# A new stream order for a hybrid decoder step, and a second copy of the last norm's scale

## The chip, the cores and the metric

The kernel runs on one core of one Trainium2 chip. The metric is the device time of one execution in microseconds (us). Three runs of the kernel before took 565.85, 564.5 and 568.01 us, median 565.85 us. All times of the trace come from one further execution, the profiled one, whose own time was 564.84 us.

## The reference

One inference step of a one-layer decoder over 256 prompt tokens and 64 sample tokens (8 sequences of 8 tokens, each with 1024 cached positions in 8 pages). Everything is float32.

```python
h = rms_norm(x, g_mix)
qa, ka, va, qs, ks, vs, ga, gs = split(h @ w_in)          # 1024 -> 5120
o_a = moba_block(rope(qa), rope(ka), va)                  # block-sparse softmax, branch 0
o_s = stick_breaking_block(qs, ks, vs)                    # branch 1
x = x + (sigmoid(ga) * (o_a @ w_branch_moba) + sigmoid(gs) * (o_s @ w_branch_sb)) @ w_out
h2 = rms_norm(x, g_ffn)
x = x + (silu(h2 @ w_ffn_gate) * (h2 @ w_ffn_up)) @ w_ffn_down
y = rms_norm(x, g_final)
```

For the sample tokens the keys and values of each branch are the cached pages (found through `page_table`) followed by the new rows. The results are `y` and the new keys and values.

## The kernel before

Activations are kept transposed, as 8 tiles of 128 features by T = 320 tokens. Every dense product is made from two roundings of each operand: a weight tile `wr` is loaded by a DMA of the SP queue (512 KB, line 157), split by ScalarE into `wh` (L152) and by VectorE into the rest `wl` (L153), and multiplied as xh·wh + xl·wh + xh·wl (L344 for the query, key and gate tiles, 24 matmul records each; L185 elsewhere). There are 3 raw buffers `wr` and 3 pairs of split ones.

The sample tokens attend to the cache in **units**: a unit is two of the eight sequences of one branch, so there are four units per branch. A unit needs four loads of cached keys (`kr`, about 1.05 MB each, four DMAs of the SP queue at L533, after a load of page numbers at L529) and four gathers of cached values (`vr`, 1.05 MB each, indirect DMAs issued by GpSimd at L541). Keys and values share one ring of 7 buffers (`RB`), so a load waits until the step that used the buffer seven loads earlier is done. Before each gather GpSimd copies one element of the key load issued last but one (`seen`, L540, `LAG` = 2); since GpSimd works in order, this holds the gather back until those keys have landed.

Up to the merge of the two branches the work is cut into steps of six **streams**, and the string `ORDER` says which stream makes its next step:

- `d`: dense work: query and key tiles, values of new tokens, first branch's output product
- `g`: gate tiles
- `s`: scores of a unit against its cached keys, in two halves (L571)
- `a`: three steps per unit: transposes of the probabilities (L659, L667; called keys step below), then the two halves of the product with the cached values (L691, 32 and 40 matmul records)
- `e`: end of a unit: its output transposed back (L704)
- `p`: attention of the prompt tokens: two score steps (L463), transposes (L504), product (L518), for two groups of heads per branch

A function is called per letter, and after each step `Loads.feed` issues what has become possible: splits of weights, one cache load at most (`PACE`), and weight loads. The list of loads follows the same string. The orders of TensorE, GpSimd and the SP queue are exactly the program's; ScalarE and VectorE are ordered by the scheduler. So a letter moved in `ORDER` moves matmuls, and with them the moments at which buffers are released and the places of DMAs in the SP queue.

After the streams come the merge, the output projection, the feed-forward part and the last norm (`last_norm`). There the scale `r` of 128 x 320 elements (the same in all partitions) is made by ScalarE and three VectorE operations, and the 8 output tiles are `xg * r`: six single tiles on VectorE, two together on GpSimd (all L854); each is then stored by a DMA of the SP or the ScalarE queue (L855).

The table of the order and the loop that reads it:

```python
for c in ORDER:
    gen, (after, mark) = self.steps.pop(c)
    ...
    step = next(gen, None)
    ...
    self.loads.feed()
```

Of the kernel before, what the change touches and what calls it, by code (L numbers as in the profile page):

```python
# [6 lines left out]
F32 = mybir.dt.float32  # L7
F32R = mybir.dt.float32r
I32 = mybir.dt.int32
AF = mybir.ActivationFunctionType  # L10
ALU = mybir.AluOpType
# [3 lines left out]
P = 128  # L15
# [4 lines left out]
T = NP_ + NS  # L20
# [13 lines left out]
SB, TB, OB, DB = 2, 3, 1, 2  # L34
# [15 lines left out]


ORDER = (
    "dddddddsddddsddsaddpsaadasegdsdaaapeddsadpsggdaappeaapdddssp"
    "gpepdgddpsagasapggegapaapgpsseggpggpdsagdasaaedgaaded"
)


# [82 lines left out]
class Net:  # L140
# [697 lines left out]
    def last_norm(self, acc, xg):  # L838

        nc, y, x1 = self.nc, self.stg, self.x1  # L840
        ps = self.pp.tile([P, T], F32, name="rb", tag="o", bufs=OB)
        nc.tensor.matmul(ps, self.ones, acc[:, 0], start=True, stop=False)
        for c in (slice(0, T // 2), slice(T // 2, T)):
            nc.tensor.matmul(ps[:, c], self.ones, acc[:, 1, c], start=False, stop=c.stop == T)
        r, w = [y.tile([P, T], F32, name=n, tag="y", bufs=3) for n in ("r", "w")]
        nc.scalar.activation(r, ps, AF.Abs_reciprocal_sqrt, scale=1.0 / D)
        nc.vector.tensor_mul(w, r, r)
        nc.vector.scalar_tensor_tensor(w, w, -0.5 / D, ps, op0=ALU.mult, op1=ALU.mult)
        nc.vector.scalar_tensor_tensor(r, w, 1.5, r, op0=ALU.add, op1=ALU.mult)
        e = 0  # L850
        for i, n in enumerate((1, 1, 1, 1, 1, 1, 2)):
            s = slice(e, e + n)
            engine = nc.gpsimd if i == 6 else nc.vector
            engine.tensor_tensor(x1[:, s], xg[:, s], r[:, None, :].to_broadcast([P, n, T]), ALU.mult)  # L854
            (nc.scalar if i % 2 else nc.sync).dma_start(self.O["y"][:, s], x1[:, s])  # L855
            e += n

# [185 lines left out]
```

## Time and profile before

| what | value |
|---|---|
| median of three runs | 565.85 us |
| profiled execution, own time | 564.84 us |
| its span | 563.0 us |
| TensorE busy | 543.2 us (96%) |
| VectorE, ScalarE, GpSimd busy | 332.7, 268.7, 48.8 us |
| HBM read | 134.22 MB |
| mean granted TensorE clock | 0.986 of full speed |

The span is what lies between the first and the last event of the core; the execution's own time is 1.8 us longer. The streams take the first 275 us of the span; in the rest TensorE is busy almost without a gap. In the profile, PE is TensorE, DVE is VectorE, ACT is ScalarE, POOL is GpSimd and SP the engine that issues most DMAs; PEclk is the share of the full clock that was granted to TensorE. A row of waits reads: total us, number of times, longest.

### The profile page before, as it was taken

Reading aid. Unit: us, or ns where it says so; the run is one execution under the profiler, and the core shown is the slowest. Engines: PE = TensorE matmul, PEld = TensorE weight load, DVE = VectorE, ACT = ScalarE, POOL = GpSimd, SP = SyncE. Lnnn points to the kernel's source line nnn. Section 1 sums busy time; section 2 is a strip of 40 time slices with the busy share of each in tenths; the row PEclk is TensorE's granted clock in tenths of the full one; section 3 lists DMA queues with packets and bytes.
Section 4 is the critical chain, followed back from the end, with each engine's and each line's share of the span. In section 5 each row is a group of like instructions: output and inputs, shape, how many; then the busy total and the mean of one; then the engine's idle time right before and its main releaser. Section 6 shows DMA issues by size and latency. Waiting matters only on the chain.

```text
span 563.0 us, 10934 instructions
## 1 busy us (share of the span) xinstructions
PE 543.2 (96%) x4252; PEld 494.0 (88%) x4252; DVE 332.7 (59%) x600; ACT 268.7 (48%) x483; POOL 48.8 (9%) x73
## 2 busy tenths in 40 slices
PE   8899999799999999999999999999999999999992
PEld 6888867578778787977999999999999999999992
DVE  6777675255575746764688656666666665444434
ACT  7775555325675444643446454444444443354321
POOL 0002102140021402131000000000000000000001
PEclk9899999799999999999999999999999999999997
DMA  8899999999699999987595544444444444544512
GB/s 306 296 374 331 368 358 405 413 392 400 225 363 357 352 401 351 383 316 293 198 325 162 150 130 151 146 150 154 149 146 152 150 152 140 153 141 144 161 33 93
DMA packets 45571, 138.86 MB, mean 247 GB/s; under 512 B 5200, under 2 KB 7504, under 8 KB 41296
## 3 DMA queue, kind: packets, MB, share of 16 engines
q1 hardware_dynamic: 40336, 104.06, 54.4%
q0 software_dynamic: 4608, 33.56, 15.0%
q8 instruction: 33, 0.54, 0.4%
q10 hardware_dynamic: 576, 0.56, 0.3%
q14 instruction: 18, 0.15, 0.1%
HBM read 134.22 MB, written 3.93 MB: 245 GB/s over the span
## 4 chain that ended last, share of the span: by engine, by line
PE 81%; DMA 7%; ACT 5%; DVE 3%; SPq 2%; issue 1%; DVEq 0%; POOL 0%; ACTq 0%
PE dps L185 55%; PE dps L344 12%; PE S L571 4%; PE po L691 4%; DMA vr<-in_cv,small 3%; DMA wr<-in_w_in 2%; ACT rot L363 2%; DMA kr<-in_ck 1%; PE dps L388 1%; PE tp L667 1%; PE dps L518 1%; PE tp L504 1%; ACT wh L152 1%; PE dps L463 1%; DVE wl L153 1%
## 5 line engine op out<-in xcount | busy, mean ns | idle before, releaser
L152 ACT ACTIVATE wh<-wr 128x1024 fp32r<-128x1024 f32 (+1 forms) x122 | 127.0, 1045 | 187.0 <-issue 110.9
L153 DVE TENSOR_TENSOR wl<-wr,wh 128x1024 fp32r<-128x1024 f32 (+1 forms) x122 | 146.8, 1205 | 76.9 <-ACT wh L152 76.7
L185 PE MATMUL dps<-x1h,wh 128*128 128x320 f32 x352 | 109.0, 310 | 0.0
L185 PE MATMUL dps<-x1l,wh 128*128 128x320 f32 x352 | 108.8, 309 | 0.0
L185 PE MATMUL dps<-x1h,wl 128*128 128x320 f32 x352 | 108.8, 309 | 0.0
L344 PE MATMUL dps<-xs,wh 128*128 128x320 f32 x256 | 78.5, 319 | 1.6 <-ACT wh L152 1.4
L344 PE MATMUL dps<-xl,wh 128*128 128x320 f32 x256 | 77.2, 314 | 0.2 <-DVE xl L307 0.2
L185 PEld LDWEIGHTS dps<-x1h,wh 128*128 128x128 f32 x352 | 66.1, 188 | 0.1
L185 PEld LDWEIGHTS dps<-x1l,wh 128*128 128x128 f32 x352 | 66.1, 188 | 0.0
L185 PEld LDWEIGHTS dps<-x1h,wl 128*128 128x128 f32 x352 | 66.1, 188 | 0.0
L185 PE MATMUL dps<-fh,wl 128*128 128x320 f32 x176 | 54.4, 309 | 0.0
L185 PE MATMUL dps<-fh,wh 128*128 128x320 f32 x176 | 54.4, 309 | 0.0
L185 PE MATMUL dps<-fl,wh 128*128 128x320 f32 x176 | 54.4, 309 | 0.0
L344 PEld LDWEIGHTS dps<-xs,wh 128*128 128x128 f32 x256 | 48.7, 190 | 4.7 <-ACT wh L152 1.5
L344 PEld LDWEIGHTS dps<-xl,wh 128*128 128x128 f32 x256 | 48.8, 191 | 0.9 <-DVE xl L307 0.9
L344 PE MATMUL dps<-xs,wl 128*128 128x320 f32 x256 | 43.6, 310 | 0.0
L344 PEld LDWEIGHTS dps<-xs,wl 128*128 128x128 f32 x256 | 39.3, 189 | 0.3 <-DVE wl L312 0.3
L541 POOL DMA_INDIRECT vr<-in_cv,small x32 | 33.3, 1040 | 43.1 <-PE po L691 11.4
L691 PE MATMUL po<-vr,pt 128*32 128x256 f32 x512 | 32.3, 394 | 4.4 <-DMA vr<-in_cv,small 4.4
L185 PEld LDWEIGHTS dps<-fh,wh 128*128 128x128 f32 x176 | 33.0, 188 | 0.0
L185 PEld LDWEIGHTS dps<-fl,wh 128*128 128x128 f32 x176 | 33.0, 188 | 0.0
L185 PEld LDWEIGHTS dps<-fh,wl 128*128 128x128 f32 x176 | 33.0, 188 | 0.0
(203 smaller groups left out, 848.9 us busy)
## 6 DMA issues: line engine op xcount, KB each, us to landing
kr<-in_ck SPq DMA_DIRECT2D x128, 256.0 KB
wr<-in_w_ff SPq DMA_DIRECT2D x44, 512.0 KB
wr<-in_w_in SPq DMA_DIRECT2D x30, 512.0 KB
wr<-in_w_down SPq DMA_DIRECT2D x16, 448.0 KB
wr<-in_w_v SPq DMA_DIRECT2D x8, 512.0 KB
wr<-in_w_b SPq DMA_DIRECT2D x8, 512.0 KB
wr<-in_w_out SPq DMA_DIRECT2D x8, 512.0 KB
wr<-in_w_down SPq DMA_DIRECT2D x8, 512.0 KB
```

The lines of the kernel that those rows point to most:

```text
L152: self.nc.scalar.activation(hi, raw, AF.Copy)
L153: self.nc.vector.tensor_tensor(lo, raw, r32(hi), ALU.subtract)
L185: nc.tensor.matmul(ps, w, x, start=first and i == 0, stop=last and i == len(todo) - 1)
L344: self.nc.tensor.matmul(ps, a, x, start=k + low + i == 0, stop=low == 1 and k + n == KD and i == n - 1)
L363: nc.scalar.activation(rot[32 * q:32 * q + 32], ps[32 * s:32 * s + 32], AF.Copy)
L388: nc.tensor.matmul(ps, self.xs[:, k], w[k][j], start=k + j == 0, stop=k + j == KD)
L463: nc.tensor.matmul(S[e][:, i], q[r, 2 * u + i, half * P:half * P + P], k[r, 2 * u + i, half * P:NP_], start=True, stop=True)
L504: nc.tensor.transpose(tp[:, i * P:(i + 1) * P], src, self.ident)
L518: nc.tensor.matmul(po[r, i, :NP_ if kt else P], t["v"][:, kt, c0:c0 + HD], mv, start=kt == 1, stop=kt == 0)
L541: self.nc.gpsimd.indirect_dma_start(out=raw.rearrange("p a b -> p (a b)"), out_offset=None, in_=self.I[f"cv{br}"], in_offset=bass.Indirect ...
L571: nc.tensor.matmul(S[r], QS[:, hp, r], raw[x][:, :, hp * P:(hp + 1) * P], start=i == 0, stop=i == 1)
L691: nc.tensor.matmul(po[r], PT[j][:, r], v[:, c:c + 256], start=j == 0, stop=j == 8)
```

## The change

Two edits. The string `ORDER` has the same letters in another order from its 19th to its 66th step. In unit 0 of the first branch, the values are multiplied directly after the scores of unit 1, ahead of a query tile of the second branch that stood there; a prompt score step moves from behind the values of unit 1 to ahead of them; the transposes of unit 2 move behind more dense work; a gate tile moves ahead of the new-value projection of the second branch. Which loads are made, and the sequence of the cache loads among themselves, stay the same; weight loads change places with them.

In `last_norm`, ScalarE copies the scale `r` into a PSUM bank (`rb`, tag `s`, which the attention scores used before). The first VectorE product still reads `r` in SBUF, the five others read the copy in the bank, GpSimd's product reads `r` in SBUF.

```diff
 ORDER = (
-    "dddddddsddddsddsaddpsaadasegdsdaaapeddsadpsggdaappeaapdddssp"
-    "gpepdgddpsagasapggegapaapgpsseggpggpdsagdasaaedgaaded"
+    "dddddddsddddsddsadpsaadasegpddsdaapdedspadasggdaappeaagdddss"
+    "pgpepdddpsagasapggegapaapgpsseggpggpdsagdasaaedgaaded"
 )
...
         nc.vector.scalar_tensor_tensor(r, w, 1.5, r, op0=ALU.add, op1=ALU.mult)
+
+        rb = self.pp.tile([P, T], F32, name="rstd3", tag="s", bufs=SB)
+        nc.scalar.activation(rb, r, AF.Copy)
         e = 0
         for i, n in enumerate((1, 1, 1, 1, 1, 1, 2)):
             s = slice(e, e + n)
-            engine = nc.gpsimd if i == 6 else nc.vector
-            engine.tensor_tensor(x1[:, s], xg[:, s], r[:, None, :].to_broadcast([P, n, T]), ALU.mult)
+            engine, v = (nc.gpsimd, r) if i == 6 else (nc.vector, rb if i else r)
+            engine.tensor_tensor(x1[:, s], xg[:, s], v[:, None, :].to_broadcast([P, n, T]), ALU.mult)
             (nc.scalar if i % 2 else nc.sync).dma_start(self.O["y"][:, s], x1[:, s])
```

On TensorE, behind the new-value projection of the first branch (`dps_903`), there stood before the query tile `dps_929` of the second branch, the prompt scores (L463), the scores `S` of unit 1 (L571, with its own keys at L615), the values `po` of unit 0 (L691) and the next query tile `dps_1108`:

```order
L344 MATMUL dps_929<-xs,wh_688 128x320
...
L344 MATMUL dps_929<-xs,wl_689 128x320 x8
L463 MATMUL dps_961<-kT_233,qT_232 128x256
...
L571 MATMUL S_984<-kr_458,QS_226 32x512 x2
...
L615 MATMUL own_995<-kT_233,QS_226 32x8 x8
L691 MATMUL po_1041<-vr_653,pt_880 32x256 x2
...
L691 MATMUL po_1041<-vs_235,pto_873 32x256 x4
L344 MATMUL dps_1108<-xs,wh_814 128x320
```

Now the same place reads, up to the first scores of unit 2 (`S_1134`):

```order
L463 MATMUL dps_923<-kT_233,qT_232 128x256
...
L571 MATMUL S_946<-kr_458,QS_226 32x512 x2
...
L615 MATMUL own_957<-kT_233,QS_226 32x8 x8
L691 MATMUL po_1003<-vr_653,pt_880 32x256 x2
...
L691 MATMUL po_1003<-vs_235,pto_873 32x256 x4
L344 MATMUL dps_1076<-xs,wh_688 128x320
...
L344 MATMUL dps_1076<-xs,wl_689 128x320 x8
L659 MATMUL tp_1111<-ident,pown_970 128x128
...
L571 MATMUL S_1134<-kr_889,QS_225 32x512 x2
```

The query tile has moved from ahead of the prompt scores to behind the values of unit 0, and one query tile fewer stands ahead of the scores of unit 2.

In the SP queue, behind the first of the four key loads of unit 2 (`kr_889`), stood a weight load `wr_959`, then the second and third key load (`kr_1027`, `kr_1058`):

```order
L157 DMA wr_827<-in_w_in 128x1024
L529 TENSOR_LOAD small
...
L533 DMA kr_889<-in_ck 128x512
...
L157 DMA wr_959<-in_w_in 128x1024
...
L533 DMA kr_1027<-in_ck 128x512
...
L533 DMA kr_1058<-in_ck 128x512
```

Now the key loads follow each other, and the weight load (`wr_1109`) comes behind the fourth:

```order
L157 DMA wr_827<-in_w_in 128x1024
L529 TENSOR_LOAD small
...
L533 DMA kr_889<-in_ck 128x512
...
L533 DMA kr_989<-in_ck 128x512
...
L533 DMA kr_1020<-in_ck 128x512
...
L533 DMA kr_1056<-in_ck 128x512
L157 DMA wr_1109<-in_w_in 128x1024
```

One weight load has moved behind three key loads; the third of them (`kr_1058` before, `kr_1020` now) is the one that GpSimd's `seen` copies read ahead of the four gathers of unit 1.

At the end of the program, ScalarE now has these rows; before, the third was not there:

```order
L246 ACTIVATE acc_5639<-x_3741 128x160 x2
L831 ACTIVATE xg<-x_3741,small 128x320
L846 ACTIVATE r<-rb 128x320
L852 ACTIVATE rstd_6371<-r 128x320
L858 DMA out_y<-x_3741 128x320 x3
```

The copy stands ahead of the three stores in ScalarE's queue.

## Prediction

> **What bounds the kernel now.** I read the page first, then TensorE's waits, then the timeline around the longest of them.
>
> ```profile
> span 563.0 us, 10934 instructions
> ...
> PE 543.2 (96%) x4252; PEld 494.0 (88%) x4252; DVE 332.7 (59%) x600; ACT 268.7 (48%) x483; POOL 48.8 (9%) x73
> ```
>
> TensorE sets the time: 19.8 us of the span are all that it is not busy. The change takes no matmul away, so it can only win what TensorE waits or runs slowly, and what lies behind its last matmul. Its waits, in total, times, longest:
>
> ```profile
> PE po L691 <- DMA vr<-in_cv,small: 4.4, 2, 3.5
> PE dps L344 <- ACT wh L152: 1.4, 1, 1.4
> ```
>
> The largest is a product with cached values that waits for its gather. TensorE's timeline shows where (start, duration):
>
> ```profile
> 95.36 1.93 PE L691 MATMUL po<-vr,pt 128*32 128x256 f32 x32
> 98.16 0.62 PE L691 MATMUL po<-vr,pt 128*32 128x256 f32 x4 [0.87 <-DMA vr<-in_cv,small]
> 102.31 1.51 PE L691 MATMUL po<-vr,pt 128*32 128x256 f32 x12 [3.53 <-DMA vr<-in_cv,small]
> ```
>
> These are the values of unit 1: the first half runs through, the second finds its third gather just late and its fourth very late. What that costs is more than the idle 4.4 us, as stretches with PE busy, granted clock and DMA show:
>
> ```profile
> 95.36:102.31 6.95, 2.56 (x37) 1.08 (x36) 2.04 (x5) 4.29 (x15) 2.29 (x4) 0.82 1.01 413
> 102.31:106.69 4.38, 4.38 (x37) 1.75 (x37) 0.00 (x0) 0.00 (x0) 0.00 (x0) 0.51 1.04 423
> 20.00:25.00 5.00, 4.52 (x20) 4.52 (x21) 4.02 (x8) 2.79 (x5) 0.00 (x0) 0.66 0.59 197
> 65.00:75.00 10.00, 10.00 (x131) 6.95 (x133) 8.34 (x18) 4.47 (x10) 0.00 (x0) 1.00 0.87 316
> 75.00:86.84 11.84, 11.84 (x97) 9.73 (x90) 6.88 (x23) 7.98 (x25) 3.25 (x6) 1.00 1.02 373
> 140.00:145.00 5.00, 5.00 (x61) 3.26 (x63) 3.61 (x8) 3.14 (x7) 0.00 (x0) 1.00 0.17 43
> ```
>
> After the wait the clock was granted by half (0.51), and the rest of the step took twice its time. The chain of waits prices the step without a wait, and shows the queues ahead of it:
>
> ```profile
> 67.83 0.33 SPq L157
> ...
> 69.33 0.34 SPq L533
> ...
> 71.37 0.37 SPq L157
> 71.78 0.88 SPq L529
> 72.93 0.33 SPq L533
> ...
> 88.11 14.16 DMA vr<-in_cv,small
> 102.31 4.44 PE po L691 x36
> ...
> 107.89 0.30 PE dps L463
> 108.53 0.37 PE tp L704 x2
> 108.90 7.04 PE dps L344 x48
> ...
> 117.80 1.73 PE po L691 x32
> ...
> 137.25 2.30 PE po L691 x40
> ```
>
> An undisturbed first half takes 1.73 us and a second half 2.30. Starting at 95.36, unit 1 would have ended at 99.39; it ended at 102.31 + 4.44 = 106.75. **The loss is 7.4 us**, and it is the most that the new order can win there.
>
> The gathers were late because they were held back. GpSimd's timeline, of the last gather of unit 0 and of the gathers of unit 1:
>
> ```profile
> 62.57 0.97 POOL L541 DMA_INDIRECT vr<-in_cv,small  x1 [5.18 <-PE tp L659]
> 82.69 0.18 POOL L540 COPY seen<-kr 1x1 f32<-1x1 f32 x1 [19.16 <-DMA kr<-in_ck]
> 83.43 0.97 POOL L541 DMA_INDIRECT vr<-in_cv,small  x1 [0.56 <-issue]
> ...
> 84.75 0.97 POOL L541 DMA_INDIRECT vr<-in_cv,small  x1 [0.16 <-issue]
> ...
> 88.11 0.97 POOL L541 DMA_INDIRECT vr<-in_cv,small  x1 [0.16 <-issue]
> ```
>
> All four wait for the third key load of unit 2 to land (82.69); the fourth is issued at 88.11 and lands 14.16 us later into DMA engines that are full (1.01 and 1.04 above).
>
> **The change: the stream order.** Three moves matter.
>
> *TensorE's arrival.* These two rows of the timeline give the old places of unit 0's values and of unit 2's first scores:
>
> ```profile
> 71.71 3.64 PE L691 MATMUL po<-vr,pt 128*32 128x256 f32 x64
> ...
> 80.41 1.92 PE L571 MATMUL S<-kr,QS 128*32 128x512 f32 x16
> ```
>
> A query tile costs 3.52 us (7.04 for 48 records). One tile fewer stands ahead of both, so TensorE gets to unit 0's values at 68.2 and to unit 2's scores at 76.9. Ahead of unit 1's values stand all the same steps and one prompt score step more (0.64, from 107.89 to 108.53): 96.0 in place of 95.36, if nothing else waits.
>
> *The keys.* SP issued the first key load of unit 2 at 69.33, the weight load at 71.37, the second key load at 72.93. Without the weight load the second follows 0.4 us sooner (0.37 and its gap). Its buffer comes from unit 1's scores, and they are done 3.5 us earlier than before, so that no wait is added on SP. In the DMA queue 0.52 MB fall away ahead of it, 1.4 us at the 373 GB/s of that stretch. So the third key load lands between 0.4 and 1.8 us sooner; I take 1.5, nearer the sum since the DMA engines are busy there: the gate opens at 81.2.
>
> *The gathers.* After the gate the first was issued 0.74 later, and the next 1.32 after it. With the same steps the fourth goes at 81.2 + 0.74 + 3 x 1.32 = 85.9, 2.2 sooner; its buffer, held by the first keys of unit 2, is released by unit 2's scores before 80.5. How fast it lands depends on who shares the engines. While the gathers ran, from 87 to 93 us, the queues of GpSimd (first row) and SP moved, in packets and MB:
>
> ```profile
> q0 software_dynamic: 247, 1.89, 74.7%
> q1 hardware_dynamic: 317, 0.58, 26.5%
> ```
>
> So a loaded SP queue leaves the gathers three quarters. The competitors are the same keys of unit 3 and weights, some a little earlier, plus the displaced weight load, which lands ahead of the gathers. I keep the 14.16 us: the fourth gather is there at 100.0, bounds 99.6 (another 0.4 from the keys that are served earlier) and 101.3 (the gate gains 0.4 and half the rest is eaten by the displaced load).
>
> *What becomes late next.* TensorE comes to unit 2's scores at 76.9 with two key loads issued only from 69.33 on. With the tail of the weight load of 67.83 they are 2.6 MB; at the 316 GB/s of this stretch that is 8.3 us, so about 77.6. Besides, the exponentials of unit 1, which the keys step needs, queue behind two weight splits of VectorE and ScalarE that used to run ahead of the scores. Neither wait is in the old trace; the one bound is zero, the other 3.5 us (the keys were there at 80.41 without a wait). I take 0.9 us for both, close to the estimate of the landing. Unit 0's fourth gather, issued at 62.57, must now be there at 68.2 + 1.73 + 0.2 = 70.1, 7.5 us after its issue; the old place shows no wait at 73.6, so the wait is between zero and 3.5; its engines had only SP's weights beside it, and I take zero.
>
> Then unit 1's values start at 96.9, the second half at 98.6, its fourth gather is wanted at 98.8 and there at 100.0: a wait of 1.2. The half ends 2.1 later, at 102.1. In the old trace this point, with the prompt step added, was 106.75 + 0.64 = 107.4. **The stream order wins 5.3 us**; the bounds are 7.4 (no wait) and 2.5 (first rival). Later steps get more lead: from 102 to 140 the old PE waited for nothing, and the DMA engines stood idle at 140 to 145 (0.17), so there is room to serve a TensorE that runs 5 us earlier. The output and feed-forward phases behind move as a block.
>
> **The change: the last norm.** Six rows carry it: ScalarE's `r`, two VectorE operations, GpSimd's product, and the chain at its end.
>
> ```profile
> 553.30 0.44 ACT L846 ACTIVATE r<-rb 128x320 f32<-128x320 f32 x1 [0.22 <-PE rb L844]
> ...
> 554.37 0.49 DVE L848 SCALAR_TENSOR_TENSOR w<-w,rb 128x320 f32<-128x320 f32 x1
> ...
> 555.70 1.60 POOL L854 TENSOR_TENSOR x<-xg,r 128x640 f32<-128x640 f32 x1 [299.98 <-DVE r L849]
> ...
> 555.83 1.82 DVE L854 TENSOR_TENSOR x<-xg,r 128x320 f32<-128x320 f32 x1
> ...
> 555.91 1.74 DVEq L1021
> 557.64 1.61 DVE x L854 x4
> ```
>
> VectorE's second product takes 1.82 us where the last four take 1.61 together: it stands while GpSimd's product runs (555.70 to 557.30). [...] An operation that reads the bank costs 0.49 (`w<-w,rb`), no more than others. ScalarE's copy costs about the 0.44 of `r`, from 555.41 to 555.87, under the first product, which keeps `r` in SBUF for that; ScalarE has nothing else, and its three stores are queued behind the copy but wait for later products anyway. Then five products run from 555.91: at 0.40 each to 557.9, at 0.49 + 0.03 to 558.5, against 559.25 (557.64 + 1.61). That is 1.3 or 0.7; I take **1.1**. GpSimd's half (557.30) is done before; its store goes behind SP's others and moves with them.
>
> **The sum.** Own time of the profiled execution 564.84 - 5.3 - 1.1 = 558.4. The median lies 1.0 above that execution; part of the spread of the three runs (3.5 us) should come from the wait that shrinks, so I add half: **558.9**.
>
> **The rivals.**
>
> *The wait stays and halves the clock again.* The gather gains only to 101.3, unit 1 waits 2.5 us, and the following 3.4 us run at half speed, which costs another 1.5: end at 101.3 + 2.1 + 1.5 = 104.9, won 2.5, with the norm 3.6. Time 561.7 (again with 0.5 for the median). For it: the engines are full, and the order cannot add bandwidth; after waits of 1.4 us and less near 20 us the clock was 0.66. [...] Chance 0.27.
>
> *The norm's copy frees nothing.* If GpSimd holds VectorE back also when one input lies in a bank, or the copy comes late, the norm wins 0: 560.0. Against it stands the duration of the bank-reading row, but GpSimd was idle then. Chance 0.09.
>
> *Slower.* TensorE now runs closer to its transfers in four places between 68 and 100 us (unit 0's values, keys step, unit 2's scores, unit 1's values). If each short wait takes the clock down, half speed could hold over most of that stretch. A halved stretch of 3.4 us loses 1.7; from the fifth on, the old loss of 7.4 and the norm's 1.1 are outweighed. With six: 10.2 and waits of 0.9, unit 1 ends at 96.0 + 11.1 + 4.0 = 111.1, 3.7 later than before; minus 1.1, time 567.9. Against it: in the trace one long wait gave one stretch of half clock, and after it 1.00. Chance 0.05.
>
> **How the numbers follow.** The forecast has 0.59; its own range is 557.0 (no wait left, median as profile) to 560.2. About 1% (5.7 us) is what a measurement of this kernel can tell from no change; faster by over 1% means below 560.2. Faster: nearly all of the forecast's cases (0.55), half of the second rival (0.04): 0.59. Slower by over 1% would be above 571.5, beyond even the price of the last rival: 0.02. Within 1%: the rest, 0.39. The range takes in the best case, 564.84 - 7.4 - 1.3 = 556.1, and the first rival with 1 us for the median: 556.2 to 562.6.
>
> **What would show it.** Right: TensorE's waits for `vr` fall from 4.4 to about 1.2; the clock of the stretch around unit 1's second half is above 0.9; GpSimd's gathers of unit 1 are issued from 82 to 86; a new wait of under 1.5 us at the scores of unit 2 or the keys step ahead of it; VectorE's second product takes about 0.5 and the last ends some 3 us after `r`. Wrong: a fourth gather still issued after 87.5, a new wait over 1.5 us at unit 0's values, a wait for `vr` or `kr` behind 107 us that gives the win back, or a second product that still takes over 1.5.

## The result, and the profile after

The changed kernel takes 559.34 us (median; 558.54 to 560.11) against 566.31 us for the kernel before, timed beside it. The ratio is 0.9877, with a 95% interval of 0.9841 to 0.9913: 1.2% faster. The prediction said 558.9 us and held the time in its range. The profiled execution took 558.79 us, 6.05 less than the one of before (564.84).

The page of the changed kernel, first its head, then TensorE's wait for the gathers of values (total us, times, longest):

```profile
span 557.0 us, 10934 instructions
...
PE 541.3 (97%) x4252; PEld 493.6 (89%) x4252; DVE 331.3 (59%) x600; ACT 269.4 (48%) x484; POOL 45.7 (8%) x73
```
```profile
PE po L691 <- DMA vr<-in_cv,small: 0.9, 1, 0.9
```

This wait has fallen from 4.4 us to 0.9. Two small waits are new, in brackets in the timeline below: for the probabilities (`p`) at the keys step of unit 1, and for the keys (`kr`) at unit 2's scores. Besides, TensorE's own busy time is 1.9 us shorter with the same 4252 matmuls: those of unit 1's second half run at the full clock where they ran at half. The stretches around these places (PE, PEld, DVE, ACT and POOL busy, granted clock, DMA share, GB/s):

```profile
75.00:80.00 5.00, 4.42 (x31) 2.09 (x29) 2.97 (x8) 2.99 (x9) 0.00 (x0) 1.00 0.93 343
...
100.00:105.00 5.00, 4.06 (x52) 2.75 (x51) 1.61 (x5) 2.28 (x6) 2.29 (x4) 1.00 1.05 413
```

The clock is 1.00 in both; before it was 0.51 from 102.31 to 106.69. From 100 to 105 us the DMA engines are as full as they were (1.05 against 1.06); from 75 to 80 us they are a little less so (0.93 against 1.02, 343 GB/s against 391). TensorE's timeline of the changed kernel, at the keys step and unit 2's scores, and at unit 1's values:

```profile
75.62 0.27 PE L659 MATMUL tp<-ident,pown 128*128 128x128 f32 x1
76.24 1.09 PE L667 MATMUL tp<-ident,p 128*128 128x128 f32 x8 [0.35 <-ACT p L642]
77.27 1.05 PE L571 MATMUL S<-kr,QS 128*32 128x512 f32 x4
78.55 1.91 PE L571 MATMUL S<-kr,QS 128*32 128x512 f32 x12 [0.23 <-DMA kr<-in_ck]
80.39 0.44 PE L704 MATMUL tp<-ident,o 128*128 128x128 f32 x2
...
97.85 2.35 PE L691 MATMUL po<-vr,pt 128*32 128x256 f32 x36
101.14 1.71 PE L691 MATMUL po<-vr,pt 128*32 128x256 f32 x26 [0.94 <-DMA vr<-in_cv,small]
...
103.42 1.53 PE L504 MATMUL tp<-ident,z 128*128 128x128 f32 x12
```

The idle times in brackets understate what such a wait costs, because the ends of matmuls are modelled and a loosely spaced group counts as busy. Counted from start to start, the keys step takes 77.27 - 75.62 = 1.65 us against 1.08 before, and the first half of unit 2's scores 80.39 - 77.27 = 3.12 against 1.86 when it waits for nothing. Unit 1's values end at 103.42, where the prediction's equivalent of the old trace stood at 107.4.

GpSimd's timeline shows when the gathers of unit 1 go, and the chain of waits how long the fourth takes:

```profile
81.32 0.18 POOL L540 COPY seen<-kr 1x1 f32<-1x1 f32 x1 [17.98 <-DMA kr<-in_ck]
82.06 0.97 POOL L541 DMA_INDIRECT vr<-in_cv,small  x1 [0.56 <-issue]
...
85.66 0.39 POOL L540 COPY seen<-kr 1x1 f32<-1x1 f32 x1
86.21 0.97 POOL L541 DMA_INDIRECT vr<-in_cv,small  x1 [0.16 <-issue]
```
```profile
86.21 14.88 DMA vr<-in_cv,small
```

The gate opens 1.37 us sooner than before (82.69), and the fourth gather goes 1.9 sooner (88.11). It takes 14.88 us to land, 0.7 longer than before.

Of the 1.9 us by which the gather goes sooner, 0.5 does not come from the gate. Before, the `seen` copy ahead of the fourth gather took 0.91 us, while VectorE split a weight tile, an operation with two SBUF inputs:

```profile
86.69 1.22 DVE L153 TENSOR_TENSOR wl<-wr,wh 128x1024 fp32r<-128x1024 f32 x1
```
```profile
87.03 0.91 POOL L540 COPY seen<-kr 1x1 f32<-1x1 f32 x1
```

The split ends at 87.91, the copy at 87.94. In the changed kernel such a split ends at 86.02 and the copy, of 0.39 us, at 86.05. Seven of the twelve traces of this case have a copy of 0.39 to 0.96 us at this place, the other five one of 0.18. Whether the split is what lengthens it was not tested.

At the end of the program, the rows of VectorE, ScalarE and GpSimd:

```profile
549.55 0.49 DVE L848 SCALAR_TENSOR_TENSOR w<-w,rb 128x320 f32<-128x320 f32 x1
550.08 0.49 DVE L849 SCALAR_TENSOR_TENSOR r<-w,r 128x320 f32<-128x320 f32 x1
...
551.08 2.08 DVE L857 TENSOR_TENSOR x<-xg,rstd 128x320 f32<-128x320 f32 x5
...
550.60 0.44 ACT L852 ACTIVATE rstd<-r 128x320 f32<-128x320 f32 x1 [1.68 <-DVE r L849]
...
550.88 1.61 POOL L857 TENSOR_TENSOR x<-xg,r 128x640 f32<-128x640 f32 x1 [300.00 <-DVE r L849]
```

Five products from the bank take 2.08 us together, and none stands still while GpSimd's product runs (550.88 to 552.49). The row `w<-w,rb` divides the whole gain in two: it starts 4.82 us earlier than before (554.37), which is what the new order won, and the span ends 7.45 after it instead of 8.63, which is what the last norm won: 1.2.

### The profile page after: what moved, and what is told of

It reads as the page before. It is cut to its first block, busy times and chain, and to the rows that moved or that the text cites. A ratio compares the mean times of both kernels' runs of the same rounds, so it can differ in the third digit from the quotient of the medians.

```text
span 557.0 us, 10934 instructions
## 1 busy us (share of the span) xinstructions
PE 541.3 (97%) x4252; PEld 493.6 (89%) x4252; DVE 331.3 (59%) x600; ACT 269.4 (48%) x484; POOL 45.7 (8%) x73
## 4 chain that ended last, share of the span: by engine, by line
PE 85%; DMA 6%; ACT 3%; DVE 2%; SPq 2%; issue 1%; POOL 1%; DVEq 0%; POOLq 0%; ACTq 0%
PE dps L185 56%; PE dps L344 12%; PE po L691 5%; PE S L571 4%; DMA vr<-in_cv,small 3%; DMA wr<-in_w_in 2%; ACT rot L363 2%; PE dps L388 1%; PE tp L667 1%; PE dps L463 1%; PE dps L518 1%; PE tp L504 1%; SPq L533 1%; DMA kr<-in_ck 1%; ACT wh L152 1%
## 5 line engine op out<-in xcount | busy, mean ns | idle before, releaser
L571 PE MATMUL S<-kr,QS 128*32 128x512 f32 x256 | 32.4, 595 | 0.8 <-ACT QS L602 0.6
```

Of the source, the lines that this page charges most:

```text
L571: nc.tensor.matmul(S[r], QS[:, hp, r], raw[x][:, :, hp * P:(hp + 1) * P], start=i == 0, stop=i == 1)
```

## The experiments

All ratios are to the kernel before, timed on the same chip beside each kernel.

**The two edits apart.** First the norm's copy alone, with the old string:

```diff
 ORDER = (
-    "dddddddsddddsddsadpsaadasegpddsdaapdedspadasggdaappeaagdddss"
-    "pgpepdddpsagasapggegapaapgpsseggpggpdsagdasaaedgaaded"
+    "dddddddsddddsddsaddpsaadasegdsdaaapeddsadpsggdaappeaapdddssp"
+    "gpepdgddpsagasapggegapaapgpsseggpggpdsagdasaaedgaaded"
 )
```

> The old stream order with the new last norm alone. My theory (GpSimd's product held VectorE's second one; a product that reads the bank is free of it): VectorE's second product takes about 0.4 to 0.5 us in place of 1.82, the stretch from the end of the norm's scale to the end of the span is 1.3 us shorter than before, and the time about 1.3 us lower, near 564.6; the wait for the values of unit 1 and the halved clock behind it stay (loss of about 7 us). Rival (the gain of the change comes all from the stream order): second product still about 1.8 us, time as before, 565.9.

Measured: 564.06 us, ratio 0.9952 (0.9933 to 0.9972). Its waits, clock and the last products:

```profile
PE po L691 <- DMA vr<-in_cv,small: 4.2, 2, 3.1
```
```profile
100.00:105.00 5.00, 2.27 (x24) 1.13 (x28) 0.32 (x2) 0.35 (x3) 1.30 (x3) 0.67 1.03 413
```
```profile
557.45 2.08 DVE L857 TENSOR_TENSOR x<-xg,rstd 128x320 f32<-128x320 f32 x5
```

The wait for the gather and the half clock stay, and the products run in the same 2.08 us. The edit does what the prediction said by itself. Its median gain (1.6 to 3.8 us by the interval) is larger than the 1.2 us that the trace accounts for; the trace shows no second place where it could come from, so the difference stays open.

Then the new string alone, with the old last norm:

```diff
-        rb = self.pp.tile([P, T], F32, name="rstd3", tag="s", bufs=SB)
-        nc.scalar.activation(rb, r, AF.Copy)
...
-            engine, v = (nc.gpsimd, r) if i == 6 else (nc.vector, rb if i else r)
-            engine.tensor_tensor(x1[:, s], xg[:, s], v[:, None, :].to_broadcast([P, n, T]), ALU.mult)
+            engine = nc.gpsimd if i == 6 else nc.vector
+            engine.tensor_tensor(x1[:, s], xg[:, s], r[:, None, :].to_broadcast([P, n, T]), ALU.mult)
```

> The new stream order with the old last norm alone. My theory: the streams end 4.6 us earlier than before, as in the trace of the change; the last norm keeps its 1.82 us product; time about 561.2 (4.7 under the kernel before). Rival (the two parts are not independent, or the norm brings most): under 2 us.

Measured: 560.86 us, ratio 0.9893 (0.9863 to 0.9924), most of the whole gain. Its waits:

```profile
PE S L571 <- DMA kr<-in_ck: 1.2, 1, 1.2
...
PE po L691 <- DMA vr<-in_cv,small: 0.3, 2, 0.2
```

The short waits are the same kind, shared out in another way: more at unit 2's scores, less at unit 1's values, and the clock between 95 and 110 us is 1.00. The gate, the fourth gather, and the second half of unit 1's values:

```profile
82.64 0.18 POOL L540 COPY seen<-kr 1x1 f32<-1x1 f32 x1 [18.98 <-DMA kr<-in_ck]
...
88.03 0.96 POOL L541 DMA_INDIRECT vr<-in_cv,small  x1 [0.16 <-issue]
```
```profile
102.19 1.71 PE L691 MATMUL po<-vr,pt 128*32 128x256 f32 x26 [0.17 <-DMA vr<-in_cv,small]
```

In this execution the new order did not bring the gate forward: it opens, and the fourth gather goes, as in the old kernel (82.69 and 88.11), and the half goes on at 102.19 where it went on at 102.31. Still the execution is 3.8 us shorter (561.01 against 564.84). Unit 1's values end at 104.47 against 106.69, or 107.33 with the prompt step added: 2.9 us won, of which 2.1 is the clock (2.28 us from 102.19 instead of 4.38 from 102.31) and 0.64 the prompt step under the wait. TensorE came to these values only at 99.67, after 1.2 us of waiting at unit 2's scores. One long wait has become short ones at two places, and no half clock followed. A sooner gate helps the changed kernel, but the gain of the order does not hang on it. Why the keys came later here is open; from 68 to 80 us the SP queue had moved 3.65 MB, against 4.04 in the trace of the changed kernel.

**The place of the copy.** The copy is still made, but in SBUF:

```diff
-        rb = self.pp.tile([P, T], F32, name="rstd3", tag="s", bufs=SB)
+        rb = y.tile([P, T], F32, name="rstd3", tag="rot", bufs=2)
```

> The changed kernel, but ScalarE's copy of the scale lies in SBUF in place of a bank; the same products read it. My theory (two SBUF inputs are excluded by GpSimd's product): the second product takes about 1.8 us again and the tail is 1.3 us longer than in the changed kernel, time about 560.6. Rival (what helped was only that GpSimd and VectorE no longer read the same tile r): second product about 0.45 us, time as the changed kernel, 559.3.

Measured: 560.66 us, ratio 0.99 (0.9869 to 0.9932), 1.3 us above the changed kernel. The two intervals overlap, so the rows have to decide. VectorE's five products behind the first:

```profile
551.23 3.33 DVE L857 TENSOR_TENSOR x<-xg,rstd 128x320 f32<-128x320 f32 x5
```

The five products take 1.25 us longer (3.33 against 2.08), and in the chain of this kernel the first of them takes 1.73 us: it ends at 552.96, after GpSimd's product (551.01 to 552.61). It is not a second copy of the scale that frees VectorE (VectorE and GpSimd read different copies here too), but the place of that copy. GpSimd's product takes 1.60 here and 1.61 in the changed kernel, so it loses nothing by VectorE's running beside it.

**The clock's share of the loss.** The old kernel, with matmuls that nothing uses put into the wait ahead of the second half of unit 1's values (six of them, which the trace shows as 12 records over 5.4 us):

```diff
+            if (br, u, half) == (0, 1, 1):
+                self.keep_warm(6)
```

> The kernel before, with six matmuls that nothing uses between the two halves of the values of unit 1, 4.4 us at full clock, in the place where TensorE waits 4.4 us. My theory (2.2 of the 7.4 us lost there are the halved clock, which comes from the wait): the clock stays at 1.00 to 107 us, the second half ends near 104.6 in place of 106.75, time about 563.8. Rival (the clock falls for another cause, or the gathers' transfers are what slows the products): clock near 0.5 and time 565.9 or more.

Measured: 563.30 us, ratio 0.9962 (0.9949 to 0.9975). The same stretch and TensorE's timeline there:

```profile
100.00:105.00 5.00, 5.00 (x48) 2.17 (x47) 0.00 (x0) 0.00 (x0) 2.28 (x4) 1.00 1.04 410
```
```profile
97.24 5.44 PE L231 MATMUL warm<-ones 128*128 128x512 f32 x12
102.61 1.93 PE L693 MATMUL po<-vr,pt 128*32 128x256 f32 x32
...
104.91 0.33 PE L659 MATMUL tp<-ident,pown 128*128 128x128 f32 x1
```

The fourth gather goes no sooner (88.11 in both traces), and the products start no sooner, at 102.61 behind the unused matmuls instead of 102.31. But they run at the full clock, and the next step starts at 104.91, where it started at 106.69 before. So of the loss of 7.4 us some 2 belong to the clock, and the gain of 1.4 to 2.9 us by the interval agrees with that.

**Which move does it.** With the bank copy kept, only the query tile moved behind unit 0's values (the prompt step and all later letters as before):

```diff
-    "dddddddsddddsddsadpsaadasegpddsdaapdedspadasggdaappeaagdddss"
-    "pgpepdddpsagasapggegapaapgpsseggpggpdsagdasaaedgaaded"
+    "dddddddsddddsddsadpsaadasegddsdaaapeddsadpsggdaappeaapdddssp"
+    "gpepdgddpsagasapggegapaapgpsseggpggpdsagdasaaedgaaded"
```

> The first part of the new order alone (values of unit 0 directly behind the scores of unit 1, one query tile later, so that a weight load falls behind the keys of unit 2), without the prompt step moved and with the old order from the values of unit 1 on; the new last norm. My theory (the third key load lands sooner, so the gathers are issued sooner): gathers issued from 82 to 86, values of unit 1 end at about 103.4 as in the changed kernel, won there 3.4 us, with the norm 4.7: time about 561.2. Rival (the later moves win most): gathers as before, time within 2 us of the norm alone, 564.

Measured: 560.67 us, ratio 0.9908 (0.9881 to 0.9935); single times from 559.5 to 563.8. Its profiled execution, with 562.8, is its second longest:

```profile
81.31 0.18 POOL L540 COPY seen<-kr 1x1 f32<-1x1 f32 x1 [18.28 <-DMA kr<-in_ck]
```
```profile
PE po L691 <- DMA vr<-in_cv,small: 2.9, 1, 2.9
```
```profile
100.00:105.00 5.00, 3.07 (x32) 1.58 (x34) 1.23 (x1) 0.91 (x1) 0.00 (x0) 0.70 1.04 426
```

The gate opens at the same moment as in the changed kernel's trace (81.31). Four of the five traces with this tile moved and the old `LAG` have it from 81.1 to 81.6 (the fifth is the stream order alone, 82.64), and the four without the move from 82.7 to 83.5: so it is this tile that brings the gate forward, though not in every execution. But the fourth gather went 0.6 us later than in the changed kernel, TensorE came to unit 1's values 1.2 us sooner (at 96.65), and a wait of 2.9 us with half clock behind it came of that. The eight executions agree with this: the two longest (562.8 and 563.8 us) have a mean granted clock of 0.989, the six others 0.992 or 0.993. This order stands on the edge of the first rival.

Only the prompt score step moved ahead of unit 1's values, bank copy kept:

```diff
-    "dddddddsddddsddsadpsaadasegpddsdaapdedspadasggdaappeaagdddss"
-    "pgpepdddpsagasapggegapaapgpsseggpggpdsagdasaaedgaaded"
+    "dddddddsddddsddsaddpsaadasegpdsdaaaeddsadpsggdaappeaapdddssp"
+    "gpepdgddpsagasapggegapaapgpsseggpggpdsagdasaaedgaaded"
```

> The old order with only the prompt score step of 0.64 us moved ahead of the values of unit 1; the new last norm. My theory: gathers as before, issued at 83.4 to 88.1 and landing at 102.3; the prompt step is hidden in the wait, 0.6 us won, and with it up to 2 if the clock is not halved; time 562.5 to 564.0, norm included. Rival (the prompt step is what the change lives from): over 4 us.

Measured: 563.03 us, ratio 0.9964 (0.9942 to 0.9987). The gate opens at 82.85 as in the old order, and the wait stays:

```profile
PE po L691 <- DMA vr<-in_cv,small: 3.6, 2, 3.1
```

Its last step of the streams starts 1.0 us earlier than the old kernel's. That is the 0.64 of work that now lies under the wait, and 0.4 from the clock, which came back sooner (the half takes 3.97 us from 102.41, instead of 4.38 from 102.31). The times alone don't show this gain: the norm's copy alone had 0.9952, inside this interval. So by the times the query tile carries most of the order's gain (0.9908), and by the trace the prompt step adds about its own length.

**What holds the gathers: the gate, or the DMA engines?** The old order with the gate one key load earlier:

```diff
-LAG = 2
+LAG = 3
```

> The kernel before, with each gather held back by the key load before the last but one (LAG 3) in place of the last but one. My theory (the gate in front of the gathers sets when they land): the gathers of unit 1 are issued about 2.7 us sooner, near 80.7, the fourth lands 2 us sooner, the loss of 7.4 us there falls to 4 or 5: time about 563. Rival (only the bytes that the DMA engines can move decide, and gathers issued sooner just push back the keys of unit 2): the wait goes to the scores of unit 2 and the time stays at 565.9.

Measured: 564.49 us, ratio 0.9978 (0.9949 to 1.0007), unclear. TensorE's waits show why a sooner gate is worth little:

```profile
PE po L691 <- DMA vr<-in_cv,small: 1.8, 2, 0.9
...
PE S L571 <- DMA kr<-in_ck: 0.7, 1, 0.7
```

The gate opens at 80.22, the fourth gather goes at 85.49 (2.6 us sooner) and is there 2.0 sooner, the clock stays at 1.00, and unit 1's values end at 102.57 instead of 106.69. But now the second half of unit 2's scores is 1.7 longer, and unit 3's values in the second branch 1.6.

The changed kernel with more work ahead of the keys step of unit 1 (a gate tile) and of unit 1's values (a dense tile):

```diff
-    "dddddddsddddsddsadpsaadasegpddsdaapdedspadasggdaappeaagdddss"
+    "dddddddsddddsddsadpsaadgasepddsddaapedspadasggdaappeaagdddss"
```

> The changed kernel with two more letters moved: gate tile 0 ahead of the keys step of unit 1 and the first scores of unit 2, and a key tile of the second branch ahead of the values of unit 1. My theory (the three waits left there, 0.6 at the keys step, 1.3 at the scores of unit 2 and 1.5 at the values of unit 1, only want more work of 3.6 us ahead of each): all three vanish, streams end 3.4 us earlier, time about 556.0. Rival (the DMA engines bind the whole stretch, so work moved ahead comes back as a wait later, at unit 2's or 3's keys or values): the same 559.3, with new waits for kr or vr between 105 and 160 us.

Measured: 558.94 us, ratio 0.9857 (0.9827 to 0.9887), which can't be told from the changed kernel. The three waits between 75 and 104 us are gone, and unit 1's values end at 103.10, 7.7 us sooner than in the old order with the two added steps counted in (106.69 + 0.64 + 3.52). TensorE's waits, and its timeline at unit 3's values:

```profile
PE po L691 <- DMA vr<-in_cv,small: 2.3, 2, 1.9
```
```profile
141.48 1.71 PE L691 MATMUL po<-vr,pt 128*32 128x256 f32 x26 [1.92 <-DMA vr<-in_cv,small]
```

There 2.5 us are given back, and 1.0 more at unit 0's values of the second branch. The wait came back behind, as the rival had it.

If the gate made these late gathers, an earlier gate would now pay. The changed kernel and the one with more cover, each with `LAG = 3`:

```diff
-LAG = 2
+LAG = 3
```

> The changed kernel with the gathers held back by the key load before last but one (LAG 3 in place of 2), so each gather may go one key load sooner. What is left in the changed kernel between 75 and 104 us are waits of 0.3 + 0.2 + 0.9 us on TensorE (the keys step, unit 2's scores, unit 1's values). Theory that the gate is still what holds the gathers: the wait of 0.9 us at unit 1's values goes (its second half falls from 3.82 to about 2.3 us) and no wait of its size appears: about 557.8. Rival, that the DMA engines' share decides and a sooner gather takes it from the keys, as in the old order with LAG 3: the wait for values goes, but one for keys of 0.7 us or more comes at the scores of unit 2, or a wait behind 200 us: 559 to 561, no gain over the changed kernel.

> The order with more cover (a gate tile and a query tile more ahead of the keys step and of unit 1's values), whose waits at 75 to 104 us were gone but which waited for gathers at the values of unit 3 of the first branch (2.5 us longer) and of unit 0 of the second (1.0), now with LAG 3. Gate theory: both waits go with gathers issued one key load sooner, 3.5 us won on 558.9: about 555.5, a version that beats the changed kernel. Rival (the DMA engines' share): these waits shrink by less than 1.5 us together or others for keys come in their place: 558 to 560.

Measured: 563.83 us, ratio 0.9973 (0.9944 to 1.0002), and 562.74 us, ratio 0.9951 (0.9929 to 0.9974). Each is about 4 us slower than with `LAG = 2`, longer than even the rival said. The changed kernel with `LAG = 3`, at unit 1's values, then its waits and the stretch ahead of the new one:

```profile
98.08 3.66 PE L691 MATMUL po<-vr,pt 128*32 128x256 f32 x64
```
```profile
PE S L571 <- DMA kr<-in_ck: 1.3, 1, 1.3
```
```profile
115.00:120.00 5.00, 5.00 (x52) 4.38 (x53) 1.80 (x3) 1.59 (x2) 0.00 (x0) 1.00 1.02 417
```

Both halves of unit 1's values run through, and the wait comes back as one for keys, at 120 us, in the second half of unit 3's scores (2.3 us longer), and as one for values at unit 3 of the second branch (1.4). The kernel with more cover waits for keys still longer:

```profile
PE S L571 <- DMA kr<-in_ck: 2.8, 2, 1.6
```

So the gate theory falls: the waits that go come back elsewhere. That a gather that goes sooner takes its time from other transfers, in stretches in which the DMA engines are full (1.02), fits this, but no run followed the single transfers. The profiled execution with `LAG = 3` took 561.2, shorter than its median; what makes the other executions up to 7 us longer is not in its trace.

## Why the prediction was right, and where its steps were off

**The gate and the gathers**: right in the trace of the changed kernel. The gate was to open at 81.2 and opened at 81.32; the gathers were to go from 82 to 86 and went from 82.06 to 86.21. The single-move kernel shows that it is the query tile that does this. But the prediction let the whole gain follow from the sooner gate, and called a fourth gather behind 87.5 a sign of being wrong; with the stream order alone it went at 88.03, and 3.8 us were won. The step from the gate to the fourth gather came out partly by luck: in the old trace it is 5.42 us (82.69 to 88.11), the long `seen` copy included, so that the same steps behind 81.2 give 86.6. The prediction took the copy at its short length, 85.9, and it took 0.39.

**No new wait at unit 0's values**: right. They start at 68.00 without one (68.2 was said).

**The clock**: right, and tested. It stays at 1.00, and the old kernel with matmuls in its wait shows the clock's share of the old loss to be about 2 us. The first rival had 0.27; what it describes does happen: the kernel with the query tile alone waited 2.9 us and had a clock of 0.70 from 100 to 105 us. The 3.4 us at half speed that it reckons with are about what the old trace has near 20 us (0.66 from 20 to 25 us, halved from 21.3 to 24.7).

**The waits that become late next**: the mechanism was right, the size was not. The prediction took 0.9 us for the keys step and unit 2's scores together; they cost 0.57 + 1.26 = 1.8. So TensorE reached unit 1's values at 97.85 and not at 96.9.

**The fourth gather**: taken as there at 100.0, it was there at 101.1. Of this 0.3 is its issue (86.21 for 85.9; a `seen` copy took 0.39 instead of 0.18), 0.7 its flight: 14.88 us against the 14.16 that was kept from the old trace. The bound of the prediction was 101.3. A gather that goes sooner flies longer in these traces: 14.16 us from 88.11 and 14.12 from 88.03 (the stream order alone), but 14.88 from 86.21 and 14.76 from 85.49 (the old order with `LAG = 3`). That it then shares full DMA engines with more that is ahead of it is the likely reason, not a shown one.

**The term of the stream order**: 5.3 us forecast. At the end of unit 1's values 107.4 - 103.42 = 4.0 had been won. Forecast and found can be set side by side: the gather 102.31 - 100.0 = 2.3, found 1.2 (the half goes on at 101.14); the clock 4.4 - 2.1 = 2.3, found 2.1 (2.28 us from 101.14 instead of 4.38); the prompt step 0.64 in both. So the mis-sized term is the gather, by half, and the clock is the largest part of what was won there. By the end of the streams it was 4.8. The other 0.8 was won behind 107 us, which the prediction left at nothing: that its 5.3 looks nearly right at the end is luck. One piece is in the list of waits: before, the second branch's new-value projection waited for ScalarE,

```profile
PE dps L388 <- ACT v L383: 0.3, 1, 0.3
```

and after there is no such row. From the start of the last matmul ahead of that step to the start of the step behind it there are now 2.10 us (153.07 to 155.17) instead of 2.64 (153.95 to 156.59). No kernel with the whole new order has this wait; the two with one move alone still have it, so another of the moved letters removes it. Which one was not tested.

**The last norm**: 1.1 us forecast, 1.2 found. The last product ends 3.1 us after `r` starts, as was said (550.08 to 551.08 + 2.08). The 1.1 took it as given that a product with one input in a bank is not held by GpSimd's product; no row of the old trace showed that. The runs do: behind the first product, the five that read the bank take 2.08 us in the changed kernel, the first three of them beside GpSimd's product (550.88 to 552.49), and 2.08 in the norm's copy alone; with the copy in SBUF they take 3.33. So the second rival (0.09) is refuted.

**Which waits the half clock followed**: between 68 and 107 us of the changed kernel none; they were 0.35, 0.23 and 0.94 us long, and the clock was 1.00. At unit 1's values it came with the 2.9 us of the single-move kernel (0.70 from 100 to 105 us) and with the waits of the norm's copy alone, the longest of 3.1 us (0.67). The row from 20 to 25 us, which the prediction counted for its first rival, is looked at in the last section.

**The sum**: 564.84 - 6.4 was to be the profiled time, 558.4; it was 558.79. The half microsecond for the median was 0.55. Both agree better than the steps do, since the 0.8 won behind 107 us nearly makes up for what the gather lacked. Two figures of the range don't come out of their own terms: the first rival with 1 us gives 564.84 - 3.6 + 1 = 562.2, not 562.6, and the best case of 556.1 lies just outside.

## What to carry to other kernels

A wait for a transfer costs its own length and can cost a stretch of half clock besides (here about 2 us on top of some 5): look at the granted clock in and behind the longest wait before you price it. Where the DMA engines are full (a share of 1.02 here), moving one transfer ahead can bring the wait back at another one (1.3 us for keys in the changed kernel with `LAG = 3`); here an order that puts work in front of the late step, and breaks the long wait into short ones, won, and an earlier gate lost some 4 us of that. When VectorE products with both inputs in SBUF run beside a GpSimd product that reads SBUF, as here, a copy of one input in a PSUM bank can be worth its 0.44 us on ScalarE if it can be made under another product: the five products took 2.08 us with the copy in the bank and 3.33 with it in SBUF.

## What the runs showed of the hardware that was not expected

In these traces the length of a single wait does not decide whether the clock falls. In the kernel with more cover, TensorE stood still for 1.9 us ahead of 141.48 (columns as above, one microsecond per row):

```profile
140.00:141.00 1.00, 0.00 (x0) 0.00 (x0) 0.00 (x0) 1.00 (x1) 0.00 (x0) 1.00 1.04 422
141.00:142.00 1.00, 0.52 (x12) 0.35 (x16) 0.00 (x0) 0.99 (x5) 0.00 (x0) 1.00 1.02 416
```

The clock stayed at 1.00. Near 20 us of the changed kernel, TensorE was idle for 0.30 + 0.83 + 0.57 = 1.7 us in three:

```profile
18.00:19.00 1.00, 0.70 (x7) 0.66 (x6) 0.78 (x2) 0.97 (x3) 0.00 (x0) 1.00 1.01 401
19.00:20.00 1.00, 0.17 (x2) 0.09 (x1) 0.79 (x6) 0.97 (x2) 0.00 (x0) 1.00 1.05 402
20.00:21.00 1.00, 0.43 (x3) 0.43 (x4) 0.45 (x1) 1.00 (x2) 0.00 (x0) 1.00 0.98 377
21.00:22.00 1.00, 1.00 (x6) 1.00 (x6) 1.00 (x2) 0.97 (x3) 0.00 (x0) 0.50 0.20 74
...
24.00:25.00 1.00, 1.00 (x7) 1.00 (x6) 0.57 (x4) 0.20 (x1) 0.00 (x0) 0.79 0.86 322
```

There the longest single wait is 1.4 us, and the clock was halved for about 3.4 us. All twelve traces of this case have that wait of 1.4 us. In nine of them a stretch of half clock follows, with 0.66 to 0.70 from 20 to 25 us; in the other three (the norm's copy alone, the stream order alone, more cover with `LAG = 3`) there is none. The stream order alone:

```profile
20.00:25.00 5.00, 4.56 (x30) 4.21 (x30) 4.02 (x8) 2.54 (x5) 0.00 (x0) 1.00 0.63 179
```

So nearly the same wait does it in one execution and not in another. The halved stretch lasts about 3.4 us here and in the single-move kernel (102.0 to 105.4), and 6.8 in and behind the long wait of the old kernel (99.8 to 106.6). What decides whether a wait brings such a stretch, and how long it lasts, was not tested.
